# A gated delta rule and attention block: preparation and outputs of the scan placed anew

## The chip, the cores and the metric

The kernel runs on one NeuronCore of a Trainium2 chip. The metric is the device time of one execution in microseconds. Five engines work side by side, each through its own queue in order: TensorE (PE; its weight loads are PEld), VectorE (DVE), ScalarE (ACT), GpSimd (POOL) and SyncE (SP), which issues the DMAs. An engine that waits for a semaphore at the head of its queue holds everything behind it.

## What is computed

One layer of a backbone with two groups of heads that read the same normalised input (512 latent and 256 context tokens, 2048 wide, fp32) through one projection. Group A, eight heads, is a chunked gated delta rule, one scan forward and one backward, whose outputs are added:

```python
qkv = silu(centred_conv(qkv, conv_w))            # 5 taps along the tokens
t_inv = triangular_solve(eye + a, eye)           # 64x64 per chunk, head, direction
u = t_inv @ (v_c * b_c)
w = t_inv @ (k_beta * exp(g_c))
def step(s, inp):
    v_new = u_i - w_i @ s
    o_i = (q_i * exp(g_i)) @ s + intra_i @ v_new
    s = s * exp(g_last) + (k_i * exp(g_last - g_i)).T @ v_new
    return s, o_i
```

Group B is grouped-query attention. Each output is gated by `silu` of a further projection, all go through one output projection and a final RMS norm.

## The kernel before, in words

Products of fp32 operands are formed from a high and a low fp32r part (`hi*hi`, `hi*lo`, `lo*hi`), three matmuls each. The stages follow each other on TensorE:

1. Modulation, norm, transposed activations, and the projections of head 0 (to about 160 us).
2. Gates and the preparation of head 0.
3. Eight scans (`gdn_scan`, scan h is head h's), from 244.9 us on. In a scan TensorE also does the next head's preparation (`gdn_prep`) and, as filler, the projections of later heads.
4. Attention, with the projections of the gates (`zl`) as filler, then the output projection.

The order on TensorE is written out by hand: the whole part is under `manual_schedule` for that engine. The other engines' instructions are put in order by a scheduler, from program order, priorities (`first_of_all()`, `tc.high_priority`) and its own estimates of time.

A scan has 12 steps, each for 128 tokens of one chunk pair: forward on one half of the partitions, backward on the other. A step has up to three slots. The first: `ksh` (k and q against the state, L712, L714; for the four context steps L717), then on VectorE `rh` (L721) and, in the eight latent steps, q's part of the output, `osbh` (L727, L730), which both read `ksh`'s tile in PSUM. The second: `tsh` (L734), then on ScalarE `vsh` and `vnh` (L738, L741). The third: the state's product (`tsh`, L745), on VectorE the new state `sth` (L750, L752), and the output's product `oh` (L756). At each slot's end the scan yields a number of columns (2700 or 3000), `pull` runs the fillers for that many (what it runs too much is kept as a debt), and at the slots listed in `PREP_AT` the preparation runs one part further.

The preparation's parts, one per entry of `PREP_AT`: transposes `t1`, `t2`, `t3` of k and q with ScalarE's copies and squares; `gq` and `gc` with VectorE's products into `gr` (decay) and `IB`; from `gr` the blocks of the triangular matrix go out to DRAM (`nd`) and come back as 16x16 blocks in `NE` (DMAs L593, L596), 14 pairs of small VectorE instructions invert them (L603, L605), they go out (`nd2`, L609) and back as `DD` (L623); meanwhile v's transposes `tv`; VectorE transposes `DD` into `DT` (L628); then `pxa`, `pxb` and two parts of `pxy` on TensorE (L636 to L675) join the blocks in `UU`, with copies on ScalarE (L653), GpSimd (L655) and VectorE (L682). `t1`, `t2`, `t3`, `gq`, `gc`, `tv` share one PSUM bank (`gtile`); `pxa`, `pxb`, `pxy` another (`PB`).

A filler projection (`proj_steps`) yields after the three products of one 128-row part: 1536 columns for q, 2304 for k and v, which have context tokens too. After the last product of a projection `conv` copies PSUM out (L182, L185), scales the first tap on ScalarE (L192), adds four taps on VectorE (L194), and tanh (L198, L199) and SiLU (L208) follow. In scans 1 to 5 a scan's fillers are one head's k, q and v, in that order.

At the end of a scan `osb` gets `o` added (L763), ScalarE squares it, GpSimd raises to the power -0.5 (L205), VectorE scales (L768), and in slot 6 of the next scan it is transposed and stored. The weights of all fillers pass through ScalarE (`whi`, L121) and GpSimd (`wlo`, L122).

## Time and profile before

| | |
|---|---|
| time, median of 3 runs | 1454.86 us (1448.2 to 1496.39) |
| the profiled execution's own time | 1453.16 us |
| its span, first to last instruction | 1451.4 us |
| mean granted clock of TensorE | 0.967 |
| TensorE busy | 1300.5 us (90%) |
| VectorE busy | 791.5 us (55%) |
| ScalarE busy | 512.2 us (35%) |
| GpSimd busy | 394.1 us (27%) |

Times are in microseconds from the span's start. In the timeline each row is one instruction or several of one kind: start, duration, engine, line, operation, what it writes and reads; in square brackets the time that its engine stood idle before it and what it waited for. In a table of waits a row says who waited for whom, then the sum, the number of times and the longest. Names lose their numbers: `ksh` is `ks` of any head. Matmuls overlap, so their starts tell the pace and not their durations. PEclk is the granted clock as a share of 2.4 GHz.

### The profile page before, as it was taken

Reading aid. Unit: us, or ns where it says so; the run is one execution under the profiler, and the core shown is the slowest. Engines: PE = TensorE matmul, PEld = TensorE weight load, DVE = VectorE, ACT = ScalarE, POOL = GpSimd, SP = SyncE. Lnnn points to the kernel's source line nnn. Section 1 sums busy time; section 2 is a strip of 40 time slices with the busy share of each in tenths; the row PEclk is TensorE's granted clock in tenths of the full one; section 3 lists DMA queues with packets and bytes.
Section 4 is the critical chain, followed back from the end, with each engine's and each line's share of the span. In section 5 each row is a group of like instructions: output and inputs, shape, how many; then the busy total and the mean of one; then the engine's idle time right before and its main releaser. Section 6 shows DMA issues by size and latency. Waiting matters only on the chain. (4 is left out here: it accounts for less than half of the span.)

```text
span 1451.4 us, 24551 instructions
## 1 busy us (share of the span) xinstructions
PE 1300.5 (90%) x9406; PEld 1041.1 (72%) x9406; DVE 791.5 (55%) x1848; ACT 512.2 (35%) x1281; POOL 394.1 (27%) x345
## 2 busy tenths in 40 slices
PE   3898897999999898988899889999898998998997
PEld 1455676888777676877777778777677777776785
DVE  3343784643767667575756555265757565533222
ACT  4111353323425243433424234243343433433221
POOL 1011201223222132222222233333333332234530
PEclk9999999999999899999989999999999999999999
DMA  9999522222222223122222353462435343474202
GB/s 305 277 287 286 135 65 57 64 78 73 60 57 57 49 56 61 49 53 64 53 56 61 70 145 92 128 220 73 145 88 140 93 119 99 154 231 138 89 27 109
DMA packets 263321, 161.93 MB, mean 112 GB/s; under 512 B 62946, under 2 KB 236091, under 8 KB 262179
## 3 DMA queue, kind: packets, MB, share of 16 engines
q1 hardware_dynamic: 263203, 160.36, 40.0%
q8 instruction: 74, 1.21, 0.3%
q14 instruction: 44, 0.36, 0.1%
HBM read 147.54 MB, written 12.77 MB: 110 GB/s over the span
## 5 line engine op out<-in xcount | busy, mean ns | idle before, releaser
L122 POOL TENSOR_TENSOR wlo_z<-wraw_z,whi_z 128x512 fp32r<-128x512 f32 x64 | 84.3, 1317 | 198.2 <-ACT whi_z L121 198.2
L158 PE MATMUL zl<-hhL,whi_z 128*128 128x512 f32 x256 | 108.6, 424 | 0.0
L158 PE MATMUL zl<-hlL,whi_z 128*128 128x512 f32 x256 | 103.4, 404 | 0.0
L158 PE MATMUL zl<-hhL,wlo_z 128*128 128x512 f32 x256 | 102.1, 399 | 0.0
L738 ACT ACTIVATE vsh<-tsh,cch 128x128 f32<-128x128 f32 x88 | 32.3, 367 | 180.9 <-PE tsh L734 180.8
L721 DVE SCALAR_TENSOR_TENSOR rh<-ksh,negeg,vtokh 64x128 f32<-64x128 f32 x176 | 61.3, 349 | 46.5 <-PE ksh L714 39.2
L139 PE MATMUL po<-wlo_wo,mh 128*128 128x512 f32 x192 | 76.9, 401 | 7.2 <-POOL wlo_wo L122 4.3
L752 DVE SCALAR_TENSOR_TENSOR sth<-sth,egl,tsh 128x128 f32<-128x128 f32 x160 | 48.5, 344 | 59.0 <-PE tsh L745 46.2
L138 PE MATMUL po<-whi_wo,mh 128*128 128x512 f32 x192 | 75.9, 398 | 2.3 <-DVE tt L211 1.2
L140 PE MATMUL po<-whi_wo,ml 128*128 128x512 f32 x192 | 76.0, 396 | 0.0
L1160 DVE SCALAR_TENSOR_TENSOR gacc<-graw,scol,gacc 128x512 f32<-128x512 f32 x60 | 52.1, 868 | 24.0 <-DMA graw<-in_w_ada 23.4
L122 POOL TENSOR_TENSOR wlo_qa<-wraw_qa,whi_qa 128x512 fp32r<-128x512 f32 x32 | 41.5, 1296 | 86.4 <-ACT whi_qa L121 74.7
L745 PE MATMUL tsh<-vsh,ktok 128*128 128x128 f32 x352 | 59.4, 295 | 0.1
L121 ACT CAST whi_z<-wraw_z 128x512 fp32r<-128x512 f32 x64 | 39.5, 618 | 54.4 <-PE zl L158 45.5
L122 POOL TENSOR_TENSOR wlo_v<-wraw_v,whi_v 128x512 fp32r<-128x512 f32 x24 | 32.6, 1358 | 95.6 <-ACT whi_v L121 87.7
L158 PEld LDWEIGHTS zl<-hhL,wlo_z 128*128 128x128 f32 x256 | 49.2, 192 | 12.0
L122 DVE TENSOR_TENSOR wlo_wo<-wraw_wo,whi_wo 128x512 fp32r<-128x512 f32 x24 | 19.7, 823 | 69.9 <-ACT whi_wo L121 67.4
L122 POOL TENSOR_TENSOR wlo_wo<-wraw_wo,whi_wo 128x512 fp32r<-128x512 f32 x24 | 34.5, 1437 | 84.3 <-ACT whi_wo L121 84.3
L158 PE MATMUL qal<-hhL,whi_qa 128*128 128x512 f32 x128 | 57.1, 446 | 0.0
L158 PEld LDWEIGHTS zl<-hhL,whi_z 128*128 128x128 f32 x256 | 49.3, 193 | 9.4 <-issue 0.8
L158 PEld LDWEIGHTS zl<-hlL,whi_z 128*128 128x128 f32 x256 | 49.5, 193 | 8.0
L745 PEld LDWEIGHTS tsh<-vsh,ktok 128*128 128x128 f32 x352 | 51.3, 203 | 5.4 <-ACT vnh L741 0.5
(393 smaller groups left out, 3902.1 us busy)
## 6 DMA issues: line engine op xcount, KB each, us to landing
wada<-in_w_ada SPq DMA_DIRECT2D x128, 256.0 KB, 5.3
wraw_z<-in_w_in SPq DMA_DIRECT2D x64, 256.0 KB, 2.9
graw<-in_w_ada SPq DMA_DIRECT2D x64, 256.0 KB, 3.0
wraw_wo<-in_w_out SPq DMA_DIRECT2D x48, 256.0 KB, 2.9
wraw_qa<-in_w_in SPq DMA_DIRECT2D x32, 256.0 KB, 2.9
wraw_q<-in_w_in SPq DMA_DIRECT2D x28, 256.0 KB, 2.8
wraw_k<-in_w_in SPq DMA_DIRECT2D x28, 256.0 KB, 2.9
wraw_v<-in_w_in SPq DMA_DIRECT2D x28, 256.0 KB, 2.8
```

The lines of the kernel that those rows point to most:

```text
L121: S.copy(hi, raw)
L122: (lo_eng or G).tensor_tensor(out=lo, in0=raw, in1=hi, op=ALU.subtract)
L138: T.matmul(out, lhsT=lh, rhs=rh, start=start, stop=False, skip_group_check=True)
L139: T.matmul(out, lhsT=lh, rhs=rl, start=False, stop=False, skip_group_check=True)
L140: T.matmul(out, lhsT=ll, rhs=rh, start=False, stop=stop, skip_group_check=True)
L158: T.matmul(pl, lhsT=lw, rhs=rt[0][:, k], start=st, stop=sp, skip_group_check=True)
L721: V.scalar_tensor_tensor(out=r[rows], in0=ks[rows, d], scalar=gsc["negeg"][rows, gcol:gcol + 1], in1=vtok[rows, p], op0=ALU.mult, op1=ALU.add)
L738: S.activation(vs, ts[:, 2], AF.Copy, scale=cc[:, 2, w:w + 1])
L745: T.matmul(ts[:, half], lhsT=ktok[:, p, half], rhs=vs, start=True, stop=True, skip_group_check=True)
L752: V.scalar_tensor_tensor(out=sn[:, d], in0=st[:, d], scalar=egl[:, half, gcol:gcol + 1], in1=ts[:, half], op0=ALU.mult, op1=ALU.add)
L1160: V.scalar_tensor_tensor(out=acc, in0=raw, scalar=scol[:, k:k + 1], in1=acc, op0=ALU.mult, op1=ALU.add)
```

## The change

1. `proj_steps` yields after each product of one operand (512 or 768 columns) instead of three; `fill` in attention counts columns and runs the same amounts.
2. `conv` adds the four taps in two segments, latent (512) and context (256), instead of over 770 columns at once.
3. In `gdn_prep` the tiles `t2`, `gq` and the first `tv` take the second PSUM bank; the subtraction of `gcum` from `gr` goes from VectorE to GpSimd.
4. `PREP_AT` moves the parts forward: v's transposes from slots 11 and 13 to 7 and 9, `gc` from 9 to 5, `pxa` from 24 to 23, the last from 31 to 29.
5. q's part of the output is written by ScalarE (L730 in the new numbering) into a tile `oq` with one half per direction; at the scan's end GpSimd adds the halves and VectorE adds `o`.

```diff
@@ proj_steps
-                for lw, first, last in ((hi[:, k4], True, False), (lo[:, k4], False, True)):
-                    for rt in ((hh, hl) if first else (hh,)):
...
-                yield 3 * (SEQ if pc is None else SEQ + CTX)
+                for lw, rt, st, sp in ((hi[:, k4], hh, k == 0, False), (hi[:, k4], hl, False, False),
+                                       (lo[:, k4], hh, False, k == KT - 1)):
+                    T.matmul(pl, lhsT=lw, rhs=rt[0][:, k], start=st, stop=sp, skip_group_check=True)
+                    if pc is not None:
+                        T.matmul(pc, lhsT=lw, rhs=rt[1][:, k], start=st, stop=sp, skip_group_check=True)
+                    yield SEQ if pc is None else SEQ + CTX
@@
+    def btile(shape, nm):
+        return PB.tile(shape, F32, tag="b", name=nm)
@@ conv
-        for j in range(1, 5):
-            V.scalar_tensor_tensor(out=acc, in0=raw[:, j:j + n], scalar=w(j), in1=acc,
-                                   op0=ALU.mult, op1=ALU.add)
+        for i0, m in ((off, SEQ), (0, CTX))[:1 if pc is None else 2]:
+            for j in range(1, 5):
+                x = acc[:, i0:i0 + m]
+                V.scalar_tensor_tensor(out=x, in0=raw[:, i0 + j:i0 + j + m], scalar=w(j), in1=x,
+                                       op0=ALU.mult, op1=ALU.add)
@@ gdn_prep
-        t2 = gtile([128, 4, 128], f"t2{nm}")
+        t2 = btile([128, 4, 128], f"t2{nm}")
...
-        V.tensor_tensor(out=gr, in0=gr, in1=gsc["gcum"][:, col].unsqueeze(2).to_broadcast([128, 12, 64]),
+        G.tensor_tensor(out=gr, in0=gr, in1=gsc["gcum"][:, col].unsqueeze(2).to_broadcast([128, 12, 64]),
                         op=ALU.subtract)
...
-        gq = gtile([128, 4, 2, 64], f"gq{nm}")
+        gq = btile([128, 4, 2, 64], f"gq{nm}")
...
-            tv_ = gtile([128, n, 128], f"tv{nm}_{p0_}")
+            tv_ = (btile if n == 2 else gtile)([128, n, 128], f"tv{nm}_{p0_}")
@@ gdn_scan
-        osb = gp2.tile([128, 4, 128], F32, tag="osb", bufs=1, name=f"osb{nm}")
+        oq = gp2.tile([128, 2, 4, 128], F32, tag="oq", bufs=1, name=f"oq{nm}")
+        osb = oq[:, 0]
...
-                    for (rows, _), d in zip(halves, (db, dt_)):
-                        eg = gsc["egsw"][rows, gcol:gcol + 1]
-                        if v == 0:
-                            V.tensor_scalar(out=osb[rows, p - 2], in0=ks[rows, d], scalar1=eg, scalar2=None,
-                                            op0=ALU.mult)
-                        else:
-                            V.scalar_tensor_tensor(out=osb[rows, p - 2], in0=ks[rows, d], scalar=eg,
-                                                   in1=osb[rows, p - 2], op0=ALU.mult, op1=ALU.add)
+                    with tc.high_priority(offset=1000):
+                        for (rows, _), d in zip(halves, (db, dt_)):
+                            S.activation(oq[rows, v, p - 2], ks[rows, d], AF.Copy,
+                                         scale=gsc["egsw"][rows, gcol:gcol + 1])
...
-        V.tensor_tensor(out=osb, in0=osb, in1=o, op=ALU.add)
+        G.tensor_tensor(out=oq[:, 1], in0=osb, in1=oq[:, 1], op=ALU.add)
+        V.tensor_tensor(out=osb, in0=oq[:, 1], in1=o, op=ALU.add)
@@
-    PREP_AT = (0, 2, 4, 6, 9, 11, 13, 24, 26, 29, 31)
+    PREP_AT = (0, 1, 2, 3, 5, 7, 9, 23, 25, 27, 29)
```

Three places of the order, in scan 3 or at its end; a digit after `h`, before the underscore, is the head (`sth4_0` is step 0 of head 4), line numbers are each kernel's own, and `x2` is two instructions.

First place: VectorE at the end of scan 3 and the start of scan 4. `cacc_v5` is v's convolution, `msh3` the mean square of head 3's output, `sth4_0` the first state of scan 4. Before:

```order
L763 TENSOR_TENSOR osbh3_5329<-osbh3_5329,oh3_5606 128x512
L549 TENSOR_TENSOR grh5_6221<-grh5_6221,cmain_77 128x384
L194 SCALAR_TENSOR_TENSOR cacc_v5_6183<-craw1_1461,cvT_80,cacc_v5_6183 128x770
L766 SCALAR_TENSOR_TENSOR msh3_6170<-msh3_6170,sqh3_4548 128x4
L194 SCALAR_TENSOR_TENSOR cacc_v5_6183<-craw1_1461,cvT_80,cacc_v5_6183 128x770
L750 COPY sth4_0_6239<-tsh4_0_6211 128x128 x2
L768 TENSOR_TENSOR osbh3_5329<-osbh3_5329,msh3_6170 128x512
L194 SCALAR_TENSOR_TENSOR cacc_v5_6183<-craw1_1461,cvT_80,cacc_v5_6183 128x770
L721 SCALAR_TENSOR_TENSOR rh4_1_6248<-ksh4_6210,negeg_87,vtokh4_5594 64x128 x2
```

The scaling of the previous output (L768) stood behind two taps and the state's copy. Now:

```order
L764 TENSOR_TENSOR oqh3_5368<-oqh3_5368,oh3_5668 128x512
L767 SCALAR_TENSOR_TENSOR msh3_6217<-msh3_6217,sqh3_4547 128x4
L769 TENSOR_TENSOR oqh3_5368<-oqh3_5368,msh3_6217 128x512
L198 SCALAR_TENSOR_TENSOR cacc_v5_6231<-craw1_1461,cvT_80,cacc_v5_6231 128x512
L750 COPY sth4_0_6287<-tsh4_0_6259 128x128 x2
L198 SCALAR_TENSOR_TENSOR cacc_v5_6231<-craw1_1461,cvT_80,cacc_v5_6231 128x512
L198 SCALAR_TENSOR_TENSOR cacc_v5_6231<-craw1_1461,cvT_80,cacc_v5_6231 128x256
L198 SCALAR_TENSOR_TENSOR cacc_v5_6231<-craw1_1461,cvT_80,cacc_v5_6231 128x512
L725 SCALAR_TENSOR_TENSOR rh4_1_6307<-ksh4_6258,negeg_87,vtokh4_5566 64x128 x2
```

The scaling (L769) stands ahead of the first tap and of the state's copy, and three taps stand between that copy and `rh4_1`.

Second place: the inverse's first product in scan 3. TensorE before, from `tsh` of step 8:

```order
L734 MATMUL tsh3_8_5848<-rh3_8_5835,UU1_2018 128x128
L158 MATMUL vl5_5809<-hhL_70,whi_v5_0_5813 128x512
L160 MATMUL vx5_5810<-hhC_75,whi_v5_0_5813 128x256
L158 MATMUL vl5_5809<-hlL_71,whi_v5_0_5813 128x512
L160 MATMUL vx5_5810<-hlC_76,whi_v5_0_5813 128x256
L158 MATMUL vl5_5809<-hhL_70,wlo_v5_0_5814 128x512
L160 MATMUL vx5_5810<-hhC_75,wlo_v5_0_5814 128x256
L636 MATMUL pxah4_5860<-DTh4_5682,grh4_5341 32x32 x2
```

TensorE now, from `ksh` of step 8 (`tsh` of step 8 comes behind the `pxah4` matmuls):

```order
L716 MATMUL ksh3_5369<-sth3_7_5868,kq3_3924 128x128
L718 MATMUL ksh3_5369<-sth3_7_5868,kq3_3924 128x128
L156 MATMUL vl5_5856<-hlL_71,whi_v5_0_5860 128x512
L158 MATMUL vx5_5857<-hlC_76,whi_v5_0_5860 128x256
L156 MATMUL vl5_5856<-hhL_70,wlo_v5_0_5861 128x512
L158 MATMUL vx5_5857<-hhC_75,wlo_v5_0_5861 128x256
L156 MATMUL vl5_5856<-hhL_70,whi_v5_0_5860 128x512
L158 MATMUL vx5_5857<-hhC_75,whi_v5_0_5860 128x256
L156 MATMUL vl5_5856<-hlL_71,whi_v5_0_5860 128x512
L158 MATMUL vx5_5857<-hlC_76,whi_v5_0_5860 128x256
L639 MATMUL pxah4_5893<-DTh4_5649,grh4_5380 32x32 x2
```

And VectorE there now, where the transpose of `DDh4` (L631) is what `pxah4` waits for, behind `cacc_q5`, q's convolution, and its SiLU:

```order
L752 SCALAR_TENSOR_TENSOR sth3_7_5868<-sth3_6_5807,egl_90,tsh3_7_5835 128x128 x2
L198 SCALAR_TENSOR_TENSOR cacc_q5_5847<-craw0_1460,cvT_80,cacc_q5_5847 128x512 x2
L725 SCALAR_TENSOR_TENSOR rh3_8_5878<-ksh3_5369,negeg_87,vtokh3_4677 64x128 x2
L198 SCALAR_TENSOR_TENSOR cacc_q5_5847<-craw0_1460,cvT_80,cacc_q5_5847 128x512 x2
L211 SCALAR_TENSOR_TENSOR kq5_5702<-craw0_1460,cacc_q5_5847 128x4x64 x2
L631 STREAM_TRANSPOSE DTh4_5649<-DDh4_5648 128x384
```

TensorE comes to `pxah4` one slot earlier in step 8; VectorE still has the four taps and both SiLUs ahead of the transpose, as before, without `osbh` between them.

Third place: ScalarE around step 9 of scan 3. Before:

```order
L121 CAST whi_v5_3_6102<-wraw_v5_3_6100 128x512
L199 ACTIVATE craw0_1460<-cacc_q5_5800 128x512
L738 ACTIVATE vsh3_9_6009<-tsh3_9_6007,cch3_4558 128x128
L741 ACTIVATE vnh3_9_6011<-tsh3_9_6007,cch3_4558 128x128
L653 COPY UU0_1430<-DDh4_5681 32x6x32 x4
L121 CAST whi_k6_0_6199<-wraw_k6_0_6197 128x512
```

The four copies out of `DDh4` (L653) came behind `vsh` and `vnh` of step 9. Now:

```order
L741 ACTIVATE vnh3_8_5947<-tsh3_8_5943,cch3_4557 128x128
L121 CAST whi_v5_3_6177<-wraw_v5_3_6175 128x512
L656 COPY UU0_1430<-DDh4_5648 32x6x32 x3
L730 ACTIVATE oqh3_5368<-ksh3_5369,egsw_89 64x128 x2
L656 COPY UU0_1430<-DDh4_5648 32x6x32
L738 ACTIVATE vsh3_9_6052<-tsh3_9_6050,cch3_4557 128x128
L741 ACTIVATE vnh3_9_6054<-tsh3_9_6050,cch3_4557 128x128
```

The copies (L656) and the two `oqh` stand ahead of `vsh` of step 9.

## Rows read from the trace of the kernel before

**Rows 1.** The page: busy time of each engine, and two groups of instructions.

```profile
PE 1300.5 (90%) x9406; PEld 1041.1 (72%) x9406; DVE 791.5 (55%) x1848; ACT 512.2 (35%) x1281; POOL 394.1 (27%) x345
...
L738 ACT ACTIVATE vsh<-tsh,cch 128x128 f32<-128x128 f32 x88 | 32.3, 367 | 180.9 <-PE tsh L734 180.8
...
L721 DVE SCALAR_TENSOR_TENSOR rh<-ksh,negeg,vtokh 64x128 f32<-64x128 f32 x176 | 61.3, 349 | 46.5 <-PE ksh L714 39.2
```

**Rows 2.** Busy time in stretches: PE, PEld, DVE, ACT, POOL, PEclk, DMA; scans 2, 6.

```profile
441.20:523.40 82.20, 73.54 (x696) 61.97 (x695) 54.81 (x148) 30.89 (x92) 20.34 (x18) 0.94 0.24 55
...
769.10:844.80 75.70, 70.47 (x666) 58.16 (x666) 43.88 (x131) 27.40 (x82) 21.15 (x19) 0.95 0.33 76
```

**Rows 3.** Waits of TensorE in scan 2: us in total, times, longest.

```profile
PE pxah L636 <- DVE DTh L628: 2.8, 1, 2.8
PE ksh L712 <- DVE osbh L727: 2.6, 1, 2.6
PE tsh L734 <- DVE rh L721: 2.1, 4, 0.7
```

**Rows 4.** The same two waits over the whole span.

```profile
PE pxah L636 <- DVE DTh L628: 23.7, 7, 6.8
...
PE ksh L712 <- DVE osbh L727: 12.9, 5, 2.6
```

**Rows 5.** TensorE in three stretches of scan 2: busy, granted clock, DMA.

```profile
479.50:486.30 6.80, 6.05 (x20) 0.52 0.14 39
486.30:495.50 9.20, 9.13 (x54) 1.00 0.49 92
500.00:503.40 3.40, 3.40 (x15) 0.54 0.02 5
```

**Rows 6.** Timeline of TensorE in scan 2: start, duration, what, idle before.

```profile
470.48 0.40 PE L158 MATMUL ql<-hlL,whi_q 128*128 128x512 f32 x1
470.71 0.39 PE L158 MATMUL ql<-hhL,wlo_q 128*128 128x512 f32 x1
...
478.06 0.49 PE L712 MATMUL ksh<-sth,kq 128*128 128x128 f32 x2 [2.58 <-DVE osbh L727]
...
498.40 0.22 PE L636 MATMUL pxah<-DTh,grh 32*32 32x32 f32 x2 [2.85 <-DVE DTh L628]
```

**Rows 7.** Timeline of VectorE, q's convolution in scan 2.

```profile
491.79 1.53 DVE L194 SCALAR_TENSOR_TENSOR cacc_q<-craw,cvT,cacc_q 128x512 f32<-128x512 f32 x2
...
496.52 1.33 DVE L208 SCALAR_TENSOR_TENSOR kq<-craw,cacc_q 128x256 f32<-128x256 f32 x2 [0.37 <-ACT craw L199]
497.78 0.56 DVE L628 STREAM_TRANSPOSE DTh<-DDh 128x384 f32<-128x384 f32 x1
```

**Rows 8.** Timeline of VectorE at the start of scan 3.

```profile
525.28 0.16 DVE L766 SCALAR_TENSOR_TENSOR msh<-msh,sqh 128x4 f32<-128x4 f32 x1
...
526.34 0.48 DVE L750 COPY sth<-tsh 128x128 f32<-128x128 f32 x2
527.32 0.69 DVE L768 TENSOR_TENSOR osbh<-osbh,msh 128x512 f32<-128x512 f32 x1 [0.50 <-POOL msh L205]
```

**Rows 9.** Line 205, GpSimd's power: ns shortest, median, longest; first and last start.

```profile
L205 POOL TENSOR_TENSOR msh<-msh,expo x8: 1007/1769/1772, 317.8 to 923.9; 128x4 f32<-128x4 f32 x8
L205 POOL TENSOR_TENSOR hss<-hss,expo x7: 1007/1007/1008, 952.1 to 1184.5; 128x4 f32<-128x4 f32 x7
```

**Rows 10.** Timeline of VectorE in scan 2: a step of the inverse, L645.

```profile
479.32 0.21 DVE L605 TENSOR_TENSOR NEh<-NEh,tmh 96x50 f32<-96x50 f32 x1
...
506.45 0.59 DVE L645 COPY_PREDICATED DDh<-cmain,pxbh 128x384 f32<-128x384 uint32 x1 [1.60 <-PE pxbh L643]
```

**Rows 11.** Timeline of ScalarE in scan 2: the four copies out of `DD`.

```profile
507.44 1.46 ACT L653 COPY UU<-DDh 32x192 f32<-32x192 f32 x4
```

**Rows 12.** Lines 546 and 211: VectorE's subtraction, a 128x512 product on GpSimd.

```profile
L546 DVE TENSOR_TENSOR grh<-grh,gcum x8: 950/958/1577, 189.4 to 762.4; 128x768 f32<-128x768 f32 x8
...
L211 POOL TENSOR_TENSOR rt<-qn,tabq x7: 1293/1303/1308, 953.9 to 1186.3; 128x512 f32<-128x512 f32 x7
```

More of the change, by code (lines that the diff above doesn't have):

```diff
@@ L153, in proj_steps @@
                 k = kq * 4 + k4
-                for lw, first, last in ((hi[:, k4], True, False), (lo[:, k4], False, True)):
-                    for rt in ((hh, hl) if first else (hh,)):
-                        st = k == 0 and first and rt is hh
-                        sp = k == KT - 1 and last
-                        T.matmul(pl, lhsT=lw, rhs=rt[0][:, k], start=st, stop=sp, skip_group_check=True)
-                        if pc is not None:
-                            T.matmul(pc, lhsT=lw, rhs=rt[1][:, k], start=st, stop=sp, skip_group_check=True)
-                yield 3 * (SEQ if pc is None else SEQ + CTX)
+                for lw, rt, st, sp in ((hi[:, k4], hh, k == 0, False), (hi[:, k4], hl, False, False),
[4 more added lines that the diff above has]
+                    yield SEQ if pc is None else SEQ + CTX
     es_g = ExitStack()
@@ L190, in w @@
             return cvT[:, j * 24 + t:j * 24 + t + 1]
+        e = raw[:, 2:]
         S.activation(acc, raw[:, 0:n], AF.Copy, scale=w(0))
-        for j in range(1, 5):
-            V.scalar_tensor_tensor(out=acc, in0=raw[:, j:j + n], scalar=w(j), in1=acc,
-                                   op0=ALU.mult, op1=ALU.add)
-        e = raw[:, 2:]
+        for i0, m in ((off, SEQ), (0, CTX))[:1 if pc is None else 2]:
[3 more added lines that the diff above has]
+                                       op0=ALU.mult, op1=ALU.add)
         if pc is not None:
@@ L1171, in build @@
     gen = fillers()
+    owed = [0]
     def fill(n):
-        for _ in range(n):
-            next(gen, None)
+        owed[0] += n * 3 * SEQ
+        while owed[0] > 0:
+            c = next(gen, None)
+            if c is None:
+                owed[0] = 0
+                return
+            owed[0] -= c
     qt = A["qt"]
```

## The prediction

> **What bounds the kernel now.** I read the page's busy times first: TensorE is busy for 1300.5 us of a span of 1451.4 us, VectorE for 791.5 us, ScalarE for 512.2 us [rows 1]. So TensorE sets the end, and a change elsewhere pays only where TensorE stands still or runs at a low clock. Then the busy times by stage: in scan 2, from 441.2 to 523.4 us, TensorE is busy for 73.5 of 82.2 us at a mean granted clock of 0.94; in scan 6 the clock is 0.95 over 75.7 us [rows 2]. The change touches the scans; first projection, attention and output run as before, apart from the cut of the fillers.
>
> The waits of TensorE in scan 2 [rows 3] are: 2.8 us at `pxah` (the first product of the preparation's inverse, released by VectorE's transpose L628), 2.6 us at `ksh` (released by `osbh` L727, which reads the same tile), and four waits for `rh` of 2.1 us together. Over the run the first has 23.7 us in 7 waits and the second 12.9 us in 5 [rows 4]: the second occurs in scans 1 to 5, the first in scans 1 to 6 and once, longer, before scan 0. I call scans 1 to 5 the five alike scans.
>
> Each of the two long waits is paid twice. Behind the wait for `osbh` TensorE ran 6.8 us at a granted clock of 0.52; between the two it had 1.00; behind the wait for the transpose 3.4 us at 0.54 [rows 5, 6]. That is half of 2.4 GHz, so the first stretch loses about 6.8 x 0.48 = 3.3 us and the second 3.4 x 0.46 = 1.6 us. One such scan therefore holds 7.5 us in these three waits and 4.9 us of clock.
>
> The Trainium skill ("TensorE: Matmul & The Clock Gate", section "What's actually happening") says to model the ramp as under 1% of a typical kernel's span. The scan's clock of 0.94 differs, so the measurement decides. By the page the clock terms below would drop out, and the sum would be 1453.2 + 5 x 2.6 + 0.6 = 1467 us.
>
> **The change, part by part.** Durations are of the profiled execution (1453.16 us, 1.8 us more than its span); the median of the runs shown is 1454.86 us, 1.7 us above it.
>
> *Projections in single operands.* The same matmuls in the same order; only the places at which they are cut change. At full clock a 512-column matmul starts every 0.23 us [rows 6], so 2304, 2560 and 3072 columns are 1.04, 1.15 and 1.4 us. A slot was 2304 or 4608 columns of k or v and is now 2304 or 3072. In sum nothing.
>
> *q's part of the output on ScalarE.* 16 VectorE instructions per scan of L721's shape (0.35 us each [rows 1]) leave; 16 on ScalarE and one add on GpSimd come. What they gain: `ksh` of step 6 no longer stands behind L727, which waited in VectorE's queue behind k's convolution and its SiLU. It then waits only for the state, which needs about 0.2 us more than TensorE: -2.4 us, and about -0.4 us of the wait for `rh` behind it. Together -2.8.
>
> *Preparation earlier.* The inverse's chain starts about 4 slots sooner, but its end does not follow. On VectorE the transpose L628 still stands behind q's four taps and two SiLUs, as the second place in the order shows, and that convolution starts when q's projection ends, where it always did. In the trace: taps from 491.79, SiLUs from 496.52 (behind ScalarE's tanh), transpose from 497.78 to 498.34 [rows 7]. Two `osbh` (0.7 us) leave that stretch, and the taps start some 0.3 us sooner: it ends near 497.4. TensorE came to `pxah` at 498.40 - 2.85 = 495.55 [rows 6]. Now `pxah` is one slot earlier: between q's last column and it stand 6144 columns instead of 9216 (-1.4 us) and no step-8 product with its wait for `rh` (about -0.5 us), so TensorE is there at 493.65. The wait is 3.75 us in place of 2.85; with half a microsecond either way 3.3 to 4.4. I take +1.1. The cover that this wait lacks is the slot that was taken away. In scan 6 no convolution of q stands there, and its wait of 2.7 us, the seventh of rows 4, goes.
>
> *Start of a scan.* New on VectorE (first place in the order): the previous head's scaling (L768, now L769) stands ahead of the first tap of v and of the state's copy. It waits for GpSimd's power: 1.77 us in most of its 8 executions, 1.01 us for the same shape elsewhere [rows 8, 9]. Queued behind it are tap, state copy and `rh`, and TensorE waits for these. The copy ended at 526.82. Now: the small L766 can start by about 525.0, then 0.16 + 1.01 + 0.69, a tap of 512 columns (0.73 [rows 7]) and the copy's 0.48 end at 528.1. TensorE was ready for the first `ksh` at about 526.8 and is now later by 0.35 (more columns) and 0.45 (the second transposes): 527.6. Wait 0.5 us, or 1.3 us with the long power; I take +0.8. Then `rh` has three taps ahead of it (0.73 + 0.4 + 0.73, the middle one by columns) and its own 0.7: 2.6 us behind the copy, against some 1.6 us of work on TensorE: 1.0, +0.5 on today's. The next state stands behind four half taps, four SiLUs and one product: by the same walk +0.7 (0 to 1.2). The output's squares now wait for GpSimd's add and come before v's copy out of PSUM, which frees the tile for the next k: +0.2. Together +2.2; at least 0.5, at most 3.6.
>
> *Taps in segments.* Eight instructions per k or v instead of four, and shorter blocks; but in the new order the 28 small steps of the inverse (0.21 us [rows 10]) stand between them, ahead of the `rh` of steps 5 to 7. Ahead of step 7 that is six steps and a SiLU, some 1.5 us, against 1.15 us of filler from a `ksh` that itself came late: 0.7. For the three I take 1.7 in all, +1.0 over what is there now (0 to 2).
>
> *Diagonal blocks on ScalarE.* The third place in the order: three copies out of `DD`, both `oqh` and the fourth copy now stand ahead of `vsh` of step 9. Behind `pxbh` (about 1.0) come 0.59 (L645), 0.70 (`rh`), 0.56 (a transpose), 4 x 0.365 [rows 10, 11], 2 x 0.35 and 0.37 for `vsh`: 5.4 us. TensorE has 1.0 + 0.4 + 1.4 + 0.15 + 1.04 + 0.3 = 4.3 us of its own until it needs it. +1.1 (0 to 1.5). The price of an `oqh` isn't in the trace; between nothing (if all hides) and 0.37 (`vsh`, twice the partitions [rows 1]) I take VectorE's own 0.35.
>
> *Two banks; the subtraction on GpSimd.* The early transposes stand on other banks, but no wait of TensorE in rows 3 is for one: nothing. The subtraction (0.96 us on VectorE) becomes about 768/512 x 1.3 = 1.95 us on GpSimd [rows 12], with 1 to 2 us of room before the last state: 0 to +0.6, I take 0. L546 itself took 0.95 us at best and 1.58 at worst [rows 12]. The Trainium skill ("GPSIMD Engine Reference", section "Specifications") has GpSimd contend with VectorE instructions that read two SBUF inputs, which speaks against this edit. By that rule the subtraction and the add would each hold one VectorE instruction by those 0.6 us, 6 us more in five scans; what stands beside them on VectorE mostly reads PSUM, so I leave it out of the sum.
>
> **The sum.** Waits per alike scan: -2.8 + 1.1 + 2.2 + 1.0 + 1.1 = +2.6. Clock: the stretch behind `osbh` goes (-3.3); the one behind `pxah` may grow from 1.6 to 3.3 lost, half of that, +0.9: -2.4. So +0.2, five times +1.0. Scan 6: -2.7 for `pxah`, -3.8 for its clock (0.05 x 75.7), +2.2 + 1.1 for the new waits: -3.2. Everything: 1453.2 - 2.2 = 1451.0, and with the 1.7 us to the median 1453 us. That is no difference: 2% of the median, 29 us, is about what a measurement of this kernel can tell from none.
>
> **Rivals.**
> - *Only the gain comes.* VectorE's queue flows better than my walk says, because it has lost 5.6 us of `osbh` and 0.96 us of subtraction per scan: the new waits at the start, at steps 5 to 7 and behind `pxbh` stay away. For it: VectorE is busy for 55 of 82 us only [rows 2]. Against: the order, in which VectorE and ScalarE wait at the head of their queues. Per scan -2.8 + 1.1 - 3.3 (no growth behind `pxah`) = -5.0, five times -25, scan 6 -6.5: 1454.9 - 31.5 = 1423 us. Faster.
> - *VectorE held at the head of its queue.* The inverse's first instruction now stands ahead of state 4 and of k's first tap, and its data come back over two DMA hops. If they come 2 us late and the power takes 1.77 us, that is 2.7 us more of waits, and where waits bunch, one more stretch at half clock as behind `osbh`, 3.3 us: +6 per scan, five times 30, 1483 to 1486 us. It decides from about 2 us of lateness. For it: nothing else stands in the queue there to fill the time. Against: by my walk the data arrive within 0.5 us of need.
> - *The change doesn't free `ksh`.* The `oqh` of step 6 stands on ScalarE behind k's tanh, which waits for VectorE's taps. If it comes as late as L727 did, 2.6 us and the clock's 3.3 come back: 1453 + 5 x 5.9 = 1482 us. Against: the tanh waits only for the 512-column part, which ends before the next state.
>
> **How the numbers follow.** Forecast (within a few us per scan of zero) 0.57; the first rival 0.23; the second 0.12; the third 0.08. The first ends over 2% faster nearly always, the second and third over 2% slower more often than not, with a small part of the forecast on either side: faster 0.23, within 2% 0.60, slower 0.17. The forecast's own bounds are 1435 to 1472; the range goes out to the rivals, 1422 to 1483.
>
> **What would show it.** Right: no wait at `ksh` for the output's reader in scans 1 to 5; at `pxah` 3.3 to 4.4 us in scans 1 to 5 and nothing in scan 6; new waits of 0.5 to 1.3 us at the first `ksh` and `rh` of a scan and at step 9's state product; scans still 81 to 83 us long, at a clock of 0.95 to 0.97. Wrong: no wait at `pxah` at all (then scans of about 75 us), or a clock below 0.94.

## The result and the profile after

The changed kernel takes 1436.68 us (median of 5 runs, 1432.96 to 1438.24) against 1454.86 us: ratio 0.9888, 95% interval 0.9848 to 0.9927. The ratio is of means and leaves out one slow run of the kernel before, 1496.39 us. Run once more it gave 0.9901 (0.9869 to 0.9933). That is within 2%, as forecast, but 14 to 16 us faster and not 2, and both intervals exclude 1.

The page's busy times, and the two GpSimd and ScalarE groups that the change touches (times in ns: shortest, median, longest):

```profile
PE 1281.4 (90%) x9406; PEld 1023.9 (72%) x9406; DVE 754.9 (53%) x1776; ACT 562.8 (39%) x1409; POOL 415.1 (29%) x361
```

```profile
L208 POOL TENSOR_TENSOR msh<-msh,expo x8: 1014/1016/1017, 312.9 to 905.6; 128x4 f32<-128x4 f32 x8
```

```profile
L730 ACT ACTIVATE oqh<-ksh,egsw x128: 357/363/366, 265.8 to 900.3; 64x128 f32<-64x128 f32 x128
```

TensorE does the same 9406 matmuls in 19 us less busy time: they ran at a higher clock (mean granted clock 0.983, before 0.967). Where, the stretches of scans 1, 2, 4 and 6 show (columns as in [rows 2]):

```profile
361.35:441.01 79.66, 71.75 (x697) 60.26 (x695) 48.99 (x138) 37.47 (x106) 22.15 (x20) 0.96 0.24 57
441.01:520.25 79.24, 71.00 (x694) 59.44 (x695) 49.82 (x140) 37.45 (x106) 22.14 (x20) 0.98 0.24 57
...
599.42:679.77 80.35, 72.10 (x695) 60.50 (x695) 49.80 (x140) 37.47 (x106) 22.13 (x20) 0.96 0.24 56
...
759.19:829.94 70.75, 67.68 (x658) 55.48 (x658) 37.85 (x117) 31.53 (x90) 22.45 (x21) 1.00 0.38 96
```

Scans 1 to 5 have a mean of 79.6 us where they had 81.5 (both from the start of one scan's first `ksh` to the next), scan 6 has 70.8 where it had 76.7: 9.6 + 6.0 = 15.5 us of the 20.2 by which the span is shorter. The profiled execution is the fastest of the five; the second profile of the same kernel (changed_again below), the slowest of its four, has the same 79.6 and 70.8 us. The other 4.6 us lie ahead of scan 1 and behind scan 6; there the second profile differs from the first by 3.5 us at the start of scan 0 (248.9 and 245.4), so I explain nothing by them.

The waits of TensorE in scan 2, beside [rows 3]:

```profile
PE pxah L639 <- DVE DTh L631: 3.6, 1, 3.6
PE tsh L734 <- DVE rh L725: 1.9, 3, 1.2
PE ksh L716 <- DVE sth L752: 1.0, 2, 0.8
PE ksh L721 <- DVE sth L752: 0.8, 1, 0.8
PE kx L158 <- ACT craw L183: 0.7, 1, 0.7
```

The wait for the output's reader is gone, the one at `pxah` is longer, and new short ones stand at the states. Their sum is 8.1 us; it was 8.6. So the waits hardly changed: what changed is the clock behind them. TensorE around its one long wait, in three stretches:

```profile
487.60:491.40 3.80, 0.45 (x52) 0.45 (x54) 2.50 (x5) 1.17 (x3) 0.00 (x0) 1.00 0.14 40
491.40:494.80 3.40, 3.40 (x74) 3.04 (x64) 0.56 (x1) 0.63 (x2) 0.00 (x0) 0.52 0.02 5
494.80:500.00 5.20, 5.20 (x126) 4.59 (x124) 2.48 (x6) 1.96 (x5) 1.28 (x1) 0.99 0.20 54
```

Behind the wait the granted clock is 0.52, half of 2.4 GHz, for 3.4 us, and nowhere else in the scan; before, one scan had two such stretches [rows 5]. In scans 1 and 4 of this profile the stretch lasts 6.8 us.

The start of scan 3 on VectorE, beside [rows 8]:

```profile
517.06 0.16 DVE L767 SCALAR_TENSOR_TENSOR msh<-msh,sqh 128x4 f32<-128x4 f32 x1 [2.89 <-ACT och L766]
518.35 0.69 DVE L769 TENSOR_TENSOR oqh<-oqh,msh 128x512 f32<-128x512 f32 x1 [1.13 <-POOL msh L208]
518.96 0.75 DVE L198 SCALAR_TENSOR_TENSOR cacc_v<-craw,cvT,cacc_v 128x512 f32<-128x512 f32 x1
519.62 0.48 DVE L750 COPY sth<-tsh 128x128 f32<-128x128 f32 x2
```

The scan's first `ksh` starts at 520.25, behind the state's copy without a wait. The mean square stands 2.6 us ahead of that copy; before, it stood 1.1 us ahead of it [rows 8].

### The profile page after: what moved, and what is told of

Same layout as the page of the kernel before. It is cut to its first block, busy times and chain, and to the rows that moved or that the text cites. A ratio compares the mean times of both kernels' runs of the same rounds, so it can differ in the third digit from the quotient of the medians.

```text
span 1431.2 us, 24720 instructions
## 1 busy us (share of the span) xinstructions
PE 1281.4 (90%) x9406; PEld 1023.9 (72%) x9406; DVE 754.9 (53%) x1776; ACT 562.8 (39%) x1409; POOL 415.1 (29%) x361
## 5 line engine op out<-in xcount | busy, mean ns | idle before, releaser
L122 POOL TENSOR_TENSOR wlo_z<-wraw_z,whi_z 128x512 fp32r<-128x512 f32 x64 | 87.0, 1360 | 195.2 <-ACT whi_z L121 195.2
L730 ACT ACTIVATE oqh<-ksh,egsw 64x128 f32<-64x128 f32 x128 | 46.4, 363 | 105.7 <-DVE rh L725 100.5
L122 POOL TENSOR_TENSOR wlo_qa<-wraw_qa,whi_qa 128x512 fp32r<-128x512 f32 x32 | 41.4, 1293 | 76.2 <-ACT whi_qa L121 63.4
L122 POOL TENSOR_TENSOR wlo_q<-wraw_q,whi_q 128x512 fp32r<-128x512 f32 x24 | 32.7, 1364 | 100.9 <-ACT whi_q L121 87.1
L122 POOL TENSOR_TENSOR wlo_v<-wraw_v,whi_v 128x512 fp32r<-128x512 f32 x24 | 31.2, 1301 | 101.0 <-ACT whi_v L121 84.3
L122 POOL TENSOR_TENSOR wlo_wo<-wraw_wo,whi_wo 128x512 fp32r<-128x512 f32 x24 | 34.4, 1436 | 83.9 <-ACT whi_wo L121 83.9
L122 DVE TENSOR_TENSOR wlo_wo<-wraw_wo,whi_wo 128x512 fp32r<-128x512 f32 x24 | 19.5, 816 | 69.9 <-ACT whi_wo L121 67.4
```

What stands on the lines that cost most here:

```text
L122: (lo_eng or G).tensor_tensor(out=lo, in0=raw, in1=hi, op=ALU.subtract)
L730: S.activation(oq[rows, v, p - 2], ks[rows, d], AF.Copy, scale=gsc["egsw"][rows, gcol:gcol + 1])
```

## The experiments

For each run: its ratio to the kernel before on the same chip, and from its profile the mean length of scans 1 to 5, split as TensorE sees it: its waits, what the clock lost (the time below full clock, weighted by the missing share), and the rest, taken as its work at full clock. Each profile is one execution (q_alone's is the second slowest of its ten, q_on_vector's the fastest of its four). The split counts the clock too high and the rest too low by the same amount: between scans 1 to 5 of one profile, over all fourteen, the rest is on average 0.27 us lower for each us of clock lost. In q_and_cut it is 70.0 us in the scans with none lost, 69.7 with 1.7 us and 69.1 with 5.1 us.

| kernel | ratio (95%) | scans 1-5 | waits | clock | rest | scan 6 |
|---|---|---|---|---|---|---|
| before | 1 | 81.5 | 8.2 | 4.8 | 68.5 | 76.7 |
| changed | 0.9888 (0.9848-0.9927) | 79.6 | 8.1 | 2.4 | 69.1 | 70.8 |
| q_alone | 1.0004 (0.9982-1.0027) | 81.3 | 9.0 | 2.7 | 69.6 | 78.5 |
| q_on_vector | 0.9881 (0.9831-0.9932) | 78.4 | 8.0 | 1.7 | 68.7 | 70.7 |
| prep_at_before | 0.9949 (0.9929-0.997) | 80.1 | 8.0 | 2.4 | 69.7 | 76.6 |
| whole_projections | 0.9994 (0.9965-1.0023) | 81.3 | 8.9 | 3.1 | 69.3 | 72.8 |
| whole_taps | 0.9886 (0.9843-0.993) | 79.6 | 8.3 | 2.4 | 68.9 | 70.0 |
| sub_on_vector | 0.9899 (0.9855-0.9944) | 79.8 | 8.2 | 2.4 | 69.2 | 70.6 |
| cut_alone | 0.9977 (0.9956-0.9998) | 81.0 | 9.0 | 3.1 | 68.9 | 75.5 |
| q_and_cut | 0.9934 (0.9899-0.9969) | 79.7 | 7.7 | 2.4 | 69.6 | 75.6 |
| pxa25 | 0.9833 (0.978-0.9885) | 76.8 | 6.7 | 0.3 | 69.8 | 71.2 |
| pxa25_30 | 0.9875 (0.9828-0.9921) | 77.3 | 7.1 | 0.0 | 70.2 | 71.0 |
| late_in_alike | 0.9828 (0.9803-0.9853) | 77.4 | 7.0 | 0.7 | 69.7 | 70.1 |
| changed_again | 0.9901 (0.9869-0.9933) | 79.6 | 8.1 | 2.4 | 69.1 | 70.8 |

My first theory was that the freed `ksh` is the gain. The first four runs try it.

**q_alone**: the kernel before with part 5 only.

```diff
-                    for (rows, _), d in zip(halves, (db, dt_)):
-                        V.tensor_scalar(out=osb[rows, p - 2], in0=ks[rows, d], ...)
+                    with tc.high_priority(offset=1000):
+                        for (rows, _), d in zip(halves, (db, dt_)):
+                            S.activation(oq[rows, v, p - 2], ks[rows, d], AF.Copy, ...)
...
+        G.tensor_tensor(out=oq[:, 1], in0=osb, in1=oq[:, 1], op=ALU.add)
```

> The kernel before with q's part of the output on ScalarE and nothing else of the change. Theory (the stall at ksh and the half-clock stretch behind it are what the change saves in scans 1 to 5): the wait of 2.6 us at ksh, about 0.7 us of the rh wait behind it and 3.3 us of clock go in each of the five alike scans, the wait at pxah stays near 2.9 us: scans of 75 to 77 us in place of 82, the whole near 1454 - 30 = 1424 us, below the changed kernel. First rival (ScalarE only moves the stall: its copies come behind k's tanh, which waits for VectorE's taps): ksh waits as before for another reader, scans stay at 81 to 83 us, 1450 to 1457 us. Second rival (the clock falls anyway, behind whatever wait is the longest): the ksh wait goes but a 6.8 us stretch at half clock stands behind pxah, scans of 78 to 79 us, 1435 to 1440 us.

Measured 1.0004. TensorE's waits in its scan 3:

```profile
PE tsh L731 <- DVE rh L722: 3.2, 5, 1.0
PE pxah L636 <- DVE DTh L628: 2.9, 1, 2.9
PE kx L160 <- ACT craw L182: 1.5, 1, 1.5
PE ksh L718 <- DVE sth L747: 1.3, 1, 1.3
```

The wait at `ksh` and its half-clock stretch are gone, as the theory wanted (clock lost: 2.7 us in place of 4.8), but nothing came of it: `rh` takes 3.2 us where it took 1.7 to 2.1, and the scan's start 1.3 us for the state and 1.5 us for `kx`. In the table 0.8 us of the 2.1 us of clock go to waits; about 0.6 us of the 1.1 by which the rest grows is the split's own shift, and the other 0.5 us stays open. None of the three outcomes on record is this one.

**q_on_vector**: the changed kernel with part 5 undone.

```diff
-                            S.activation(oq[rows, v, p - 2], ks[rows, d], AF.Copy, ...)
+                            V.tensor_scalar(out=osb[rows, p - 2], in0=ks[rows, d], ...)
```

> The changed kernel with q's part of the output back on VectorE, the rest of the change in place. Theory (q's part on ScalarE is what frees ksh): VectorE's queue holds the output's instructions between the inverse's steps ahead of rh of step 6, so TensorE waits 2 to 4 us at step 6 and runs at half clock behind it, +5 to +7 us per alike scan; in this order the transpose stands ahead of q's taps, so the pxah wait of 3.6 us shrinks to about 1 us and its half-clock stretch goes, -4 to -5: scans of 79 to 82 us, the whole 1430 to 1448 us, with the wait in another place. Rival (the other parts carry the gain): no wait over 1 us at step 6, scans of 74 to 75 us, the whole near 1410 us.

Measured 0.9881, the changed kernel's time. Waits in its scan 3:

```profile
PE ksh L715 <- DVE osbh L730: 5.0, 1, 5.0
PE ksh L720 <- DVE sth L755: 0.9, 1, 0.9
PE tsh L737 <- DVE rh L724: 0.8, 2, 0.5
```

`ksh` waits 5.0 us, longer than ever, and `pxah` not at all: in this order VectorE's transpose stands ahead of q's taps. One long wait took the place of the other, with one half-clock stretch of 3.4 us at its end. So part 5 is neither enough nor needed for the gain, and the first theory fell.

**prep_at_before**: the changed kernel with the old slots.

```diff
-    PREP_AT = (0, 1, 2, 3, 5, 7, 9, 23, 25, 27, 29)
+    PREP_AT = (0, 2, 4, 6, 9, 11, 13, 24, 26, 29, 31)
```

> The changed kernel with the preparation's parts at the slots of the kernel before (0 2 4 6 9 11 13 24 26 29 31). Theory (the earlier slots serve only scan 6 and the preparation before scan 0, and cost at pxah in the alike scans): scan 6 gets its pxah wait of about 2.7 us and a stretch at half clock back, +5 to +6 us; the wait before scan 0 comes back, +2 to +3 us; the alike scans lose 0.7 us of the pxah wait each and up to 1 us of waits at rh and sth, -1 to -2 each: the whole within 3 us of the changed kernel, 1430 to 1440 us. Rival (the early slots carry the gain in all scans): alike scans back at 81 to 82 us, 1448 to 1455 us.

Measured 0.9949: 1443.58 us, between the theory's range and the rival's. Scan 6 takes 76.6 us, with its `pxah` wait back, as the theory said; the alike scans stay at 80.1. Not foreseen: they do not get better by the shorter `pxah` wait, since the start of the scan pays. Waits in its scan 2:

```profile
PE pxah L639 <- DVE DTh L631: 2.9, 1, 2.9
PE tsh L734 <- DVE rh L725: 1.6, 2, 1.4
PE kx L158 <- ACT craw L183: 1.5, 1, 1.5
PE ksh L721 <- DVE sth L750: 1.2, 2, 0.6
```

`kx` waits 1.5 us (0.7 in the changed kernel) and the scan's first `ksh` 0.6 us for its state (0; the row's second 0.6 is the next scan's): with the last part at slot 31 and not 29, VectorE's copies into `UU` and its mask products stand in the output's chain.

**pxa25**: `PREP_AT` of the changed kernel with 25, 27, 29, 31 at its end.

> The changed kernel with the inverse's first product at slot 25 in place of 23 and the parts behind it at 27, 29 and 31. Theory (what is left at pxah is the time that VectorE needs for q's convolution, at which TensorE arrives 3.6 us too early): with two more slots of v's columns in front TensorE arrives within 0.5 us of the transpose; the wait falls from 3.6 to 0 to 0.7 us, the half-clock stretch behind it goes, 4.5 to 6.5 us less in each of scans 1 to 5: scans of 73 to 75 us, the whole 1402 to 1412 us. Rival (the transpose follows pxah down, since VectorE's taps are themselves held by TensorE's progress): the wait stays at 3 us or more, 1430 to 1437 us. Second rival (the late end of the preparation holds the next scan's first product): the wait at pxah goes and one of 2 us or more at the first tsh of scans 2 to 6 comes, 1420 to 1430 us.

Measured 0.9833. In scan 2 no stretch is left at half clock (clock 1.00):

```profile
442.90:518.80 75.90, 69.56 (x697) 58.09 (x695) 50.57 (x139) 37.26 (x106) 22.44 (x20) 1.00 0.26 59
```

`pxah` waits 1.2 us, for no half-clock stretch. The time is the second rival's, but its wait at `tsh` isn't there. The theory is right in its place, and half right in its size: 2.7 us per scan and not 4.5 to 6.5, because `kx` rose to 1.6 to 2.4 us; it is 1.5 to 2.5 us in every kernel here whose preparation ends at 31 and whose output is added on GpSimd, and 0.7 to 1.1 us in the others.

The second theory, then: what counts is not the sum of the waits but how many long ones a scan holds, for behind each the clock can fall; the cut of the fillers is what keeps the pieces short. The next runs undo one part each.

**whole_projections**: the changed kernel, yielding after three products.

```diff
-                    yield SEQ if pc is None else SEQ + CTX
+                yield 3 * (SEQ if pc is None else SEQ + CTX)
```

> The changed kernel with the filler projections yielding after three products again (1536 or 2304 columns). Theory (the cut only moves columns between slots; the sum is the same): scans within 0.7 us of the changed kernel's 79.6 us, the whole 1433 to 1440 us, no wait of TensorE over 1 us that the changed kernel lacks. Rival (even slots hide the VectorE instructions behind rh and the state): slots of 2304 and 4608 columns leave some steps short, the waits for rh and sth grow by 1 to 2 us per scan and bring a second stretch at half clock: scans of 81 to 83 us, 1444 to 1455 us.

Measured 0.9994: nearly the whole gain of the alike scans, 1.7 of 1.9 us, is gone with a part that I had costed at nothing, and 2.0 of the 6.0 us of scan 6. By the split the 1.7 us are 0.8 of waits, 0.7 of clock and 0.2 of rest. TensorE's waits in its scan 3, and the stretch behind the second of them:

```profile
PE pxah L641 <- DVE DTh L633: 3.6, 1, 3.6
PE tsh L736 <- DVE rh L727: 3.2, 4, 2.1
```

```profile
558.00:562.90 4.90, 2.81 (x14) 1.84 (x13) 4.82 (x15) 2.12 (x5) 1.31 (x1) 1.00 0.39 107
562.90:566.30 3.40, 3.40 (x13) 2.95 (x12) 2.29 (x12) 0.63 (x3) 0.00 (x0) 0.54 0.00 0
```

At `rh` of step 6 TensorE waits 2.1 us in one piece, and 3.4 us at a clock of 0.54 follow (in scans 3 to 5). In the changed kernel the same steps 4 to 7 hold 2.6 us of waits in four pieces, the longest 1.2, at full clock throughout. VectorE's block of taps, SiLUs and inverse steps is the same; that the even slots spread it over several steps is my reading of these rows.

**whole_taps**: the changed kernel with taps over 770 columns.

```diff
-        for i0, m in ((off, SEQ), (0, CTX))[:1 if pc is None else 2]:
-            for j in range(1, 5):
+        for j in range(1, 5):
```

> The changed kernel with the taps over all 770 columns again, four instructions per k or v. Theory (the prediction's: segments with the inverse's steps between them are late for rh in steps 5 to 7): the waits at ksh and rh of steps 4 to 7, 2.6 us per alike scan in the changed kernel, fall by 0.5 to 1.0 us, scans 1 to 5 of 78 to 79 us, the whole 1430 to 1434 us. Rival (longer taps hold more: a tap of 770 columns took 1.02 us by itself and 1.6 us beside GpSimd, where one of 512 took 0.74 us either way): rh of step 1 and of steps 5 to 7 waits 0.5 to 1.5 us more, the whole 1440 to 1446 us.

Measured 0.9886. The time is in the theory's range, the waits are not: `rh` takes 0.5 us more and the states 0.3 less, scans as long as before the edit. The segments give nothing that can be measured.

**sub_on_vector**: the changed kernel with the subtraction of `gcum` on VectorE.

```diff
-        G.tensor_tensor(out=gr, in0=gr, ...
+        V.tensor_tensor(out=gr, in0=gr, ...
```

> The changed kernel with the subtraction of gcum on VectorE again. Theory (there is room on either engine): VectorE has 0.95 us more in the last two steps of a scan, the waits for the last rh or the first state grow by at most 0.5 us: scans within 0.5 us of 79.6, the whole 1435 to 1440 us. Rival (VectorE is what TensorE waits for at the end of a scan, through the output's chain and v's copy out of PSUM): kx waits 1.5 us instead of 0.7 and the first state 0.5 us, +1.3 us per scan: 1443 to 1446 us.

Measured 0.9899: the theory, no difference (scans 0.2 us longer).

**pxa25_30**: pxa25 with 25, 27, 28, 30.

> The changed kernel with the inverse's products at slots 25, 27, 28 and 30 (they were at 23, 25, 27, 29; the run with 25, 27, 29, 31 took 0.983 of the kernel before). Theory (with the last part at 31 VectorE's copies of UU and the mask products run beside GpSimd's add, 2.1 us for 1.1, and push the output's chain and v's copy, so kx waits 1.6 to 2.4 us instead of 0.7): ended one slot earlier kx falls to 0.7 to 1.0 us, pxah stays near 1.2 us without a half-clock stretch, scans 1 to 5 of 75 to 76.5 us, the whole 1418 to 1424 us. Rival (slot 28 is too early for the copy behind pxb: pxy waits 0.7 us or more for XT's or DT's source): what kx gains is lost there, 1424 to 1430 us.

Measured 0.9875: 1431.07 us, just above the rival's range. `kx` falls to 1.0 as the theory said, but `rh` rises to 3.3 us in scan 3 (1.9 in the run with 31), so what `kx` gained is lost there, and not at `pxy`, where the rival had put it.

**cut_alone** and **q_and_cut**: the kernel before with the cut (`proj_steps` and `fill`) alone, and with the cut and part 5.

> The kernel before with the filler projections cut into single products and nothing else of the change. Theory (the cut spreads waits that would otherwise bunch, but the reader of ksh's tile on VectorE still stands behind k's convolution): ksh keeps one wait of 2 to 4 us for the output's reader and a half-clock stretch behind it, pxah its 2.9 us and its own: scans 1 to 5 of 80 to 82.5 us, the whole 1443 to 1455 us, within 0.7% of the kernel before. Rival (the cut alone carries the gain): no wait over 1.3 us before pxah, scans of 79 us, the whole near 1435 us.

> The kernel before with two parts of the change: q's part of the output on ScalarE and the projections in single products. Theory (each alone does nothing, since the wait of one moves or stays; together no wait between the scan's start and pxah is over 1.3 us and the half-clock stretch there goes): scans 1 to 5 of 79 to 80.5 us, scan 6 at 76 to 77 us with its pxah wait, the whole 0.991 to 0.995 of the kernel before. Rival (the early preparation is needed for it): a wait of 2 us or more at rh of steps 5 to 7 and two stretches at half clock, scans of 81 to 82.5 us, 0.997 to 1.003.

Measured 0.9977 and 0.9934, each in its theory's range (scan 6 of q_and_cut is 0.4 us below it). cut_alone keeps both long waits; its scan 3:

```profile
PE ksh L710 <- DVE osbh L725: 3.0, 1, 3.0
PE pxah L634 <- DVE DTh L626: 2.8, 1, 2.8
```

Ahead of `pxah`, q_and_cut has no wait over 1.6 us, and its scans 1 to 5 have a mean of 79.7 us, the changed kernel's (78.0 to 81.3 by scan). So with the old slots of the preparation these two parts make the gain of the alike scans, and only together (0.2 and 0.5 us alone, 1.8 us together). With the new slots the cut needs no part 5: q_on_vector has 78.4 us. The cut is in every kernel here that gains over 0.5 us per alike scan; scan 6, 75.6 us, needs the earlier preparation.

**late_in_alike**: the late slots in scans 1 to 5 alone; **changed_again**: the changed kernel.

```diff
+    PREP_LATE = (0, 1, 2, 3, 5, 7, 9, 25, 27, 29, 31)
...
-            prep, prep_at = gdn_prep(h + 1), PREP_AT
+            prep, prep_at = gdn_prep(h + 1), (PREP_LATE if 1 <= h <= 5 else PREP_AT)
```

> The changed kernel with the inverse's products at slots 25, 27, 29 and 31 in scans 1 to 5 alone, at 23 to 29 in scans 0 and 6. Theory (pxah's wait and its half-clock stretch in scans 1 to 5 are what the change leaves): scans 1 to 5 of 76 to 77.5 us, scan 0 near 116 us, scan 6 near 70.8 us, 14 to 18 us below the changed kernel on the same chip, near 1420 us. Rival (scan to scan the wait moves on to kx and rh as in the run that ended at 30): 5 to 10 us below it.

> The changed kernel itself once more, beside the three others on one chip. Both theories expect 0.985 to 0.992 of the kernel before; the half-clock stretch behind pxah is 3.4 us in some scans and 6.8 us in others, with scans of 79.2 and 80.4 us to match.

Measured 0.9828 and 0.9901: 1425.33 against 1436.16 us on one chip, 10.8 us less, between the theory's 14 to 18 and the rival's 5 to 10. It beats both kernels; pxa25 isn't told apart from it, and was not run beside the changed kernel on one chip. What it leaves in scans 1 to 5 is `kx`; scan 2:

```profile
PE kx L158 <- ACT craw L183: 2.4, 1, 2.4
PE tsh L734 <- DVE rh L725: 1.9, 3, 1.2
PE pxah L639 <- DVE DTh L631: 1.2, 1, 1.2
```

## Why the prediction was right, and where it was wrong

The forecast, no difference by 2%, held, and the time lies in the range. It held by the width of the 2%: the sum said 2 us less, 14 to 16 us came, midway to the first rival's 31.5, and the intervals tell them from nothing. The sum said +0.2 us per alike scan and -3.2 in scan 6; the trace says -1.9 and -6.0. Of the signs named, those at `ksh` and `pxah` came; the new waits at a scan's start and at step 9's state product did not, and the alike scans are 79.2 to 80.4 us long and not 81 to 83.

Right, with its size: `ksh`'s wait for the output's reader went (-2.6; forecast -2.8 with the `rh` behind it). At `pxah` 3.3 to 4.4 us were forecast and 3.6 came, in scans 1 to 5 and not in scan 6: the order showed that the inverse's end did not follow its start. By the split the clock gave back 2.4 us per alike scan, as forecast; with its shift of 0.27 us per us taken off it is worth about 1.8. An `oqh` takes 0.363 us (forecast 0.35), and the subtraction on GpSimd (1.47 us where 1.95 was estimated) is worth nothing either way (sub_on_vector).

Wrong, by step:

- *Projections in single operands, "in sum nothing".* This is the step that failed. Without it the changed kernel is at 0.9994. I counted columns, which do stay the same, and not that a slot of 2304 or 4608 columns leaves some steps without cover. Part of the clock in my sum hung on it: in whole_projections a stretch comes back behind `rh` of step 6 in three of five scans, on balance 0.7 of the 2.4 us are lost again, and the waits are 0.8 us longer than in the changed kernel. That kernel has scans 0.2 us shorter than before and a scan 6 4.0 us shorter, close to my sum; but its terms are not mine (waits +0.7 us for a forecast +2.6), so the nearness is luck.
- *Start of a scan, +2.2.* In scan 2 it was -0.1: `kx` 0.7 (0.8), first `ksh` 0 (0.2), `rh` 0.3 (0.5), second state 0.85 (0), third `rh` 0 (0.4). I let the mean square start where VectorE's queue had it before, and missed that a preparation that ends at slot 29 clears four `UU` copies and a mask product out of the output's way: the chain from it to the state's copy takes 2.6 us, and here the copy is done before TensorE needs it. And the power takes 1.02 us in all eight executions, where most took 1.77 [rows 9]. prep_at_before, which ends at 31, has the same 2.6 us and pays 0.8 us at `kx` and 0.6 at the first `ksh`: the mechanism was right, for another order.
- *Diagonal blocks, +1.1 at step 9.* It was 0 in the alike scans. I charged the copies with the second transpose and `rh`; they read `DD` and wait for neither. VectorE's L648 and ScalarE in scan 2:

```profile
498.00 0.59 DVE L648 COPY_PREDICATED DDh<-cmain,pxbh 128x384 f32<-128x384 uint32 x1 [1.55 <-PE pxbh L646]
...
498.62 1.08 ACT L656 COPY UU<-DDh 32x192 f32<-32x192 f32 x3 [3.10 <-DVE DDh L648]
499.71 0.74 ACT L730 ACTIVATE oqh<-ksh,egsw 64x128 f32<-64x128 f32 x2
500.48 0.35 ACT L656 COPY UU<-DDh 32x192 f32<-32x192 f32 x1
500.85 0.37 ACT L738 ACTIVATE vsh<-tsh,cch 128x128 f32<-128x128 f32 x1
```

  They start at the end of L648, which started at 498.00, and `vsh` is done 3.2 us behind that start, where my walk had 4.4; TensorE comes later.
- *Steps 4 to 7, +1.0.* It was +1.9 (2.6 us of `rh` and state waits where there had been 0.75 behind `ksh`), the one place where I was too low.
- *Scan 6, -3.2.* `pxah` -2.7 and the clock -3.4 (forecast -3.8) came; of the +3.3 for new waits nothing did (3.1 us of other waits before, 3.0 now), for the two reasons above.

In the alike scan 2 the waits thus come to -2.6 + 0.8 - 0.1 + 1.9 - 0.4 (the last `rh`) = -0.4, for a forecast of +2.6. The rest is 0.6 us longer in the table, which is the split's shift for 2.4 us of clock (0.27 x 2.4), and no sign that TensorE's own work grew. The rival "only the gain comes" (1423 us) had the sign and was right that the new waits at the start and behind `pxbh` stay away; at steps 5 to 7 they came. late_in_alike comes near its time by another way, without the long wait at `pxah`.

Of the two rules weighed, the first does not hold here as a bound on the clock terms: the ramp penalty that the Trainium skill ("TensorE: Matmul & The Clock Gate", section "What's actually happening") puts under 1% of a typical kernel's span. The five alike scans lost 5 x 4.8 = 24 us to half clock, 1.6% of the span (about 17 us, 1.2%, with the split's shift taken off), and the changed kernel lost half of that. The other, also of the Trainium skill ("GPSIMD Engine Reference", section "Specifications": GpSimd contends with VectorE instructions that read two SBUF inputs), the traces bear out. In scans 1 to 5 of the changed kernel neither the subtraction nor the add slows such an instruction (its mask products take 0.54 to 0.56 us), so to leave it out of the sum was right there. In the variants it shows. VectorE and GpSimd at the end of q_alone's scan 2, and at the end of pxa25's scan 2, where GpSimd adds the halves:

```profile
528.09 1.02 DVE L194 SCALAR_TENSOR_TENSOR cacc_v<-craw,cvT,cacc_v 128x770 f32<-128x770 f32 x1 [2.65 <-ACT cacc_v L192]
...
529.15 2.15 DVE L194 SCALAR_TENSOR_TENSOR cacc_v<-craw,cvT,cacc_v 128x770 f32<-128x770 f32 x1
...
529.19 1.29 POOL L122 TENSOR_TENSOR wlo_k<-wraw_k,whi_k 128x512 fp32r<-128x512 f32 x1 [5.35 <-ACT whi_k L121]
```

```profile
509.79 2.13 DVE L552 TENSOR_TENSOR grh<-grh,cmain 128x384 f32<-128x384 f32 x2
...
509.87 1.62 POOL L763 TENSOR_TENSOR oqh<-oqh 128x512 f32<-128x512 f32 x1
```

The same tap takes 1.02 us alone and 2.15 beside GpSimd's subtraction for the weights (L122); two mask products that take 0.55 each alone take 2.13 beside the add. In both places the slowed instruction ends 0.4 to 0.8 us behind GpSimd's. That this is what pushes `kx` in the kernels that end at 31 fits, but is not shown alone: cut_alone, which ends at 31 without GpSimd's add, has `kx` at 1.1 us and q_and_cut, with it, at 1.9, and the add's own time is in the same chain.

Still open: why the rest, with the split's shift allowed for, differs by up to 0.6 us either way from the kernel before (most in q_on_vector, below it, and in prep_at_before, above it), and how `kx` would be freed in late_in_alike. The new slots and the second PSUM bank were never tried alone; q_and_cut has neither, at the changed kernel's mean of the alike scans.

## What to carry to other kernels

Count the long waits of the bounding engine in a stage, not only their sum: here a wait of 2 us or more costs its length and up to 3.4 us of clock, one of 1.2 us only its length, so splitting or merging waits can pay where the sum stays. It need not: q_alone lost one long wait and gained nothing: new short ones came, and part of its loss stays open. Cutting filler work into even pieces can be worth more than removing a stall, and an edit that "only moves" work must be costed by what each slot covers. When an order shows something queued ahead, check what it reads before charging it with its neighbours.

## What the runs showed of the hardware

The price of a long wait is not its length. In scans 0 to 6 of the fourteen profiles, no wait of TensorE up to 1.7 us was followed by a low clock; with those from 1.8 to 5.0 us it ran at half clock for 3.4 us, for 6.8 us or not at all. In scans 1 to 6 the fall came between 1.6 us before the wait's end and 1.7 us behind it. The wait of 5.0 us in q_on_vector brought 3.4 us in all five scans; the same wait of 2.85 us at `pxah` in q_and_cut brought none in scans 1 and 2, 6.8 us in scan 3 and 3.4 in scan 4. Scan 2 with none, and scan 3 with these 6.8 us and 3.4 more behind `kx` at its end (1.9 us):

```profile
440.80:518.90 78.10, 70.10 (x695) 58.08 (x695) 51.19 (x133) 36.85 (x106) 22.14 (x19) 1.00 0.25 58
518.90:600.10 81.20, 74.08 (x694) 61.89 (x695) 51.59 (x133) 36.75 (x105) 22.15 (x19) 0.94 0.24 56
```

The same program's scans thus differ by 3.1 us with the same long waits. What decides between none, 3.4 and 6.8 us was not tried. It also goes with how far the runs of one kernel scatter: the seven of q_and_cut reach from 1430.98 us at a mean granted clock of 0.984 to 1449.79 us at 0.971.
